# Table building and chunk inputs of a hybrid S5 layer: table buffers, store queue, three matrices kept, copies shared out

## The chip, the cores and the metric

The kernel runs on one NeuronCore of one Trainium2 chip. The metric is the device time of one execution in microseconds; three executions of the kernel before are given.

## The reference

The model has two layers over 1024 latent tokens and 256 context tokens of width 1024. The change lies in layer 0, in the S5 half of its mixer. It projects the normalised tokens to 768 channels `u` (48 groups of 16 channels) and runs a complex linear recurrence of 64 states for each group, once forwards and once backwards, over context and latent tokens together:

```python
lam_bar = jnp.exp(lam * step)
b_bar = ((lam_bar - 1.0) / lam)[..., None] * lax.complex(b_re, b_im)
bu = lax.complex(jnp.einsum('btgh,gph->btgp', u, b_bar.real),
                 jnp.einsum('btgh,gph->btgp', u, b_bar.imag))
...
_, s = lax.associative_scan(_linear_recurrence, (a, bu), axis=1)
return (jnp.einsum('btgp,ghp->btgh', s.real, c_re) - jnp.einsum('btgp,ghp->btgh', s.imag, c_im))
```

After it come a gated FNet mix of 256 channels, an output projection, and a second layer (pooling and a short convolution), which the change does not touch.

## The kernel before, in words

All instructions stand in the order in which the program writes them, engine by engine; there is no scheduler. fp32 products are made from three passes over values split in a high and a low part (`mm3`, L373); the low part `wlo` of a weight is made on VectorE, or on GpSimd, the high part `whi` on ScalarE (helper `act`, L243).

The recurrence is cut into chunks of 8 tokens: 160 chunk positions forwards and as many backwards. Three kinds of data are needed:

- **Input matrices** (`bl_task`, L507 to L531), twelve of them, each for 4 groups: VectorE makes `bl` in five operations on 128x512 from `bb` and `pwb` (the powers of `lam_bar`); the second half, `pe()`, is eight transposes on TensorE (L527), two copies on ScalarE to a slot `bltw`, and a store to DRAM `bltd` on GpSimd's queue (L530).
- **Output matrices** (`cl_task`, L533 to L575), twelve: VectorE makes `cl` in five operations on 128x576, and two stores `cld` go out (L556); the `pe()` half is 32 small matmuls into `pz` (L566), ScalarE's copies to `z`, and two small VectorE operations (`dg`, `z`). After every second task `z` is put in a list, and the next `flush()` stores it (L962, `zd`). There are two `z` buffers, so the first copy to the third `z` waits until the first `zd` store has landed.
- **Chunk inputs**: the projected `u` of channel block m is stored to DRAM `ud` by three DMAs on GpSimd's queue (L1021, L1024, L1025) and read back as `ub` in another layout.

The loop over m = 0 to 5 (L988) computes the six channel blocks and their context part `uc`. Inside its matmuls the hook calls `fill()` (L960 to L978) at chosen k. A `fill` flushes `z`, runs the `pe()` half of the table task two back, and starts the VectorE half of the next. So table number t+1's VectorE work and table t-1's TensorE work stand in the same place. The buffers of `bl` (2, with scratch `blp`) lie in pool `gt`, those of `cl` (2, with scratch `clp`) in pool `kt`. `cld` and `zd` stores go on `self.sq`, which is SyncE's queue until the loop over m has ended and GpSimd's from there.

Then comes `fx(0)` (the FNet projection, eight k steps), with `hook0` (L1063) at each k: at k other than 2 and 5 it runs one `bl_mm` and one `fill`. `bl_mm(i)` (L1033 to L1050) multiplies input matrix i (`blt`, loaded back from `bltd`) with the chunk inputs `ub`: for each of two parts one PSUM tile of 3 groups and one of 1 group, which ScalarE copies to the recurrence's state (128x480 and 128x160). It ends with `bl_load(i+3)`, two loads on SyncE's queue. `bl_mm` 0 to 5 write state half `va`, 6 to 11 half `vb`. `vb` lies where pool `kt` was, so its first write waits until the last table and `z` stores have landed.

VectorE then runs, for `va`, `tree(0)` (five levels) and six steps; `tree(1)` does it for `vb`, and after that a long run of dependent steps over both halves follows. TensorE projects further channel blocks beside it. The output stage (`yps`, L1205) needs the end of that chain.

Of the kernel before, what the change touches and what calls it, by code (L numbers as in the profile page):

```python
# [9 lines left out]
F32 = mybir.dt.float32  # L10
# [7 lines left out]
P = 128  # L18
# [176 lines left out]
class Builder:  # L195
# [218 lines left out]
    def s5_prelim(self, tp, s5s, raw):  # L414
# [88 lines left out]
                    self.act(self.acf[:, o[0], o[1]], pw[:, k, 8], scale=sc)  # L503
        return tables, inputs

    def bl_task(self, b, hf):

        nc = self.nc
        g4 = slice(8 * b + 4 * hf, 8 * b + 4 * hf + 4)
        bl = self.gt.tile([P, 2, 4, 16, 8], F32, tag="bl", name="bl", bufs=2)  # L510

        def dve():
            p = self.gt.tile([P, 4, 16, 8], F32, tag="blp", name="blp", bufs=1)
            B = [x[:, g4].unsqueeze(3).to_broadcast([P, 4, 16, 8]) for x in (self.bbs, self.bb[:, 0], self.bb[:, 1])]
            W = [self.pwb[:, i, g4].unsqueeze(2).to_broadcast([P, 4, 16, 8]) for i in range(3)]
            self.mul(p, B[0], W[0])
            self.mul(bl[:, 0], B[2], W[2])
            self.mul(bl[:, 1], B[1], W[1])
            self.sub(bl[:, 0], p, bl[:, 0])
            self.add(bl[:, 1], p, bl[:, 1])  # L520

        def pe():
            blt = self.slot("bltw").rearrange("p (r g n) -> p r g n", r=2, g=4)
            for ri in range(2):
                pt = self.ps("m", "pt")
                for g in range(4):
                    nc.tensor.transpose(pt[:, g * P:g * P + P], bl[:, ri, g].rearrange("p h s -> p (h s)"),  # L527
                                        self.c("ident"))
                self.act(blt[:, ri].rearrange("p g n -> p (g n)"), pt)
            nc.gpsimd.dma_start(self.bltd[b][:, :, 4 * hf:4 * hf + 4], blt)  # L530
        return dve, pe  # L531

    def cl_task(self, b, hf):  # L533

        nc = self.nc
        g0 = 8 * b + 4 * hf
        g4 = slice(g0, g0 + 4)
        cl = self.kt.tile([P, 2, 4, 144], F32, tag="cl", name="cl", bufs=2)

        def dve():  # L540
            p = self.kt.tile([P, 4 * 144], F32, tag="clp", name="clp", bufs=1)
            p4 = p.rearrange("p (g e h) -> p g e h", g=4, e=9)
            C = [x[:, g4].unsqueeze(2).to_broadcast([P, 4, 9, 16]) for x in (self.cbs, self.cb[:, 0], self.cb[:, 1])]
            W = [self.pwc[:, i, :, g4].rearrange("p e g -> p g e").unsqueeze(3).to_broadcast([P, 4, 9, 16])
                 for i in range(3)]
            c4 = cl.rearrange("p r g (e h) -> p r g e h", e=9)
            self.mul(p4, C[0], W[0])
            self.mul(c4[:, 0], C[2], W[2])
            self.mul(c4[:, 1], C[1], W[1])
            self.sub(c4[:, 0], p4, c4[:, 0])  # L550
            cf = cl[:, 1].rearrange("p g e -> p (g e)")
            self.stt(cf, p, -1.0, cf, ALU.mult, ALU.subtract)
            for d in range(2):
                r = slice(64 * d, 64 * d + 64)
                o = 16 * (1 - d)
                self.sq.dma_start(self.cld[b][r, :, 4 * hf:4 * hf + 4], cl[r, :, :, o:o + 128])  # L556

        def pe():
            pz = [self.ps("m", "pz"), self.ps("m", "pz")]
            for q in range(4):  # L560
                for ri in range(2):
                    for d in range(2):
                        r = slice(64 * d, 64 * d + 64)
                        o = slice(0, 128) if d == 0 else slice(16, 144)
                        w = self.bb[r, ri, g0 + q:g0 + q + 2].rearrange("p g h -> p (g h)")
                        nc.tensor.matmul(pz[d][32 * q:32 * q + 32, 0:128], w, cl[r, ri, q, o],  # L566
                                         start=(ri == 0), stop=(ri == 1), skip_group_check=True)
            if hf == 0 and b > 0:
                self.z = self.kt.tile([P, 2, 240], F32, tag="z", name="z", bufs=2)
            z = self.z[:, hf]  # L570
            self.act(z[:, 0:128], pz[1][:, 0:128])
            self.act(z[:, 128:240], pz[0][:, 16:128])
            dg = self.kt.tile([P, 16], F32, tag="dg", name="dg", bufs=2)
            self.stt(dg, self.c("eye16"), self.v("d", 2 * b + hf), pz[0][:, 0:16], ALU.mult, ALU.add)
            self.add(z[:, 112:128], z[:, 112:128], dg)  # L575
            if hf == 1:
                self.zq.append((b, self.z))
        return dve, pe


# [167 lines left out]
    def layer0(self, es):  # L748
        nc, tc, A = self.nc, self.tc, self.A
# [184 lines left out]
        tables, inputs = self.s5_prelim(xp, s5s, rawb)  # L934
        rest, self.inter = self.inter, []
        for x in rest:
            if not isinstance(x, int):
                x()
        tables(0)
        inputs = inputs()  # L940
        for _ in range(4):
            next(inputs)


# [3 lines left out]
            return hh[k], hlo[k]  # L948

        todo = []  # L950
        for b in range(6):
            todo += [(self.bl_task, b, 0), (self.bl_task, b, 1)]
        for b in range(6):
            todo += [(self.cl_task, b, 0), (self.cl_task, b, 1)]
        pend = []

        self.zq = []
        self.sq = nc.sync

        def flush():  # L960
            for b, z in self.zq:
                self.sq.dma_start(self.zd[b].rearrange("a p e -> p a e"), z)  # L962
            self.zq = []

        def fill():
            flush()
            if len(pend) == 2 or not todo:
                if pend:
                    pend.pop(0)()
            if todo:  # L970
                f, b, hf = todo.pop(0)
                t = f(b, hf)
                if f == self.cl_task and b + hf == 0:
                    self.add(self.cbs, self.cb[:, 0], self.cb[:, 1])
                t[0]()
                pend.append(t[1])
# [2 lines left out]

        def bl_load(i):  # L980
            b, hf = divmod(i, 2)
            blt = self.slot("blt").rearrange("p (r g n) -> p r g n", r=2, g=4)
            nc.sync.dma_start(blt, self.bltd[b][:, :, 4 * hf:4 * hf + 4])
            ub = self.slot("ub")[:, 0:768].rearrange("p (g j) -> p g j", g=4)
            nc.sync.dma_start(ub, self.ud[b][4 * hf:4 * hf + 4].rearrange("g h s j -> (h s) g j"))
            blq.append((blt, ub))

        for m in range(6):  # L988
# [11 lines left out]
            if m == 1:  # L1000
                tables(1)
                sx.close()
                self.gt = ax.enter_context(tc.tile_pool(name="gt", bufs=1))
                self.kt = kx.enter_context(tc.tile_pool(name="kt", bufs=1, side="right"))
                self.z = self.kt.tile([P, 2, 240], F32, tag="z", name="z", bufs=2)
                self.cb = self.kt.tile([P, 2, NG, 16], F32, name="cb")
                nc.sync.dma_start(self.cb, A["s5c"])
                self.cbs = self.kt.tile([P, NG, 16], F32, name="cbs")
# [4 lines left out]
            self.mm3([(pc[:, :TC], 0, TC)], hi, lo, lambda k: (chh[k], chl[k]), 8)  # L1013
            if m == 0:
                self.w_split(names[2])
                for _ in inputs:
                    pass
            else:
                fill()
# [14 lines left out]
        def bl_mm(i):  # L1034
            blt, ub = blq.pop(0)
            for ri in range(2):
                for g0, n in ((0, 3), (3, 1)):
                    ps = self.ps("m" if n == 1 else "acc", "vps")
                    for j in range(n):
                        g = g0 + j  # L1040
                        o = slice(160 * j, 160 * j + 160)
                        nc.tensor.matmul(ps[0:64, o], blt[:, ri, g, 0:64], ub[:, g, 0:160], start=True, stop=True)
                        nc.tensor.matmul(ps[64:128, o], blt[:, ri, g, 64:128], ub[:, g, 32:192][:, ::-1],
                                         start=True, stop=True)
                    c, gl = divmod(4 * i + g0, NH)
                    dst = v[c][:, :, ri, gl:gl + n].rearrange("p i g -> p g i")
                    src = ps[:, 0:160 * n].rearrange("p (g i) -> p g i", g=n)
                    self.act(dst, src)
            if i + 3 < 12:
                bl_load(i + 3)  # L1050

        blk = list(range(12))
        self.sq = nc.gpsimd

        def fx(ct, hook):
            x = self.slot("fx")
# [4 lines left out]
            return lambda: nc.gpsimd.dma_start(xd[:, ct], x)  # L1061

        def hook0(k):  # L1063
            if k not in (2, 5):
                bl_mm(blk.pop(0))
                fill()

        fx(0, hook0)()
# [63 lines left out]
        n = NSTEP - 1  # L1132
# [6 lines left out]
        for m in range(8, 16):  # L1139
            k = m - 8  # L1140
# [90 lines left out]
        for i in range(12):  # L1231
# [19 lines left out]
            if i == 9:  # L1251
                for j, op in enumerate((ALU.add, ALU.subtract)):
                    o = 512 * j
# [26 lines left out]
        for kt in range(5):  # L1280
# [3 lines left out]
            for i in range(ni):  # L1284
                o = 512 * i if kt < 4 else 512
# [18 lines left out]
        for kt in range(4):  # L1304
            hi, lo = self.w_take(("dft", kt))
            self.w_split(("dft", kt + 1) if kt < 3 else ("glu", 0))
            for i in range(2):
                cs_ = slice(512 * i, 512 * i + 512)
                for ct in range(2):
                    cc = slice(128 * ct, 128 * ct + 128)  # L1310
                    zhh, zll = zh[:, i, kt, cc], zl[:, i, kt, cc]
                    o = pa[2 * i + ct]
# [513 lines left out]
```

## Time and profile before

| what | value |
|---|---|
| median of three executions | 913.28 us (912.3 to 913.72) |
| the profiled execution | 915.5 us |
| span of its trace | 913.7 us |
| granted TensorE clock, mean | 0.976 |
| TensorE busy | 864.6 us (95%) |
| VectorE busy | 673.0 us (74%) |
| ScalarE busy | 343.4 us (38%) |
| GpSimd busy | 94.2 us (10%) |

The engine shares are means over stages with different limits. The stage that the change touches runs from about 75 us (first channel block) to about 218 us (start of `tree(1)`); the page's 40 slices of 22.8 us each show TensorE there at 7 to 9 tenths, and the DMA engines at 9 tenths from 137 to 206 us. In every view, times count from the start of the span, and an idle time in square brackets stands with what ended it.

### The profile page before, as it was taken

Reading aid. Unit: us, or ns where it says so; the run is one execution under the profiler, and the core shown is the slowest. Engines: PE = TensorE matmul, PEld = TensorE weight load, DVE = VectorE, ACT = ScalarE, POOL = GpSimd, SP = SyncE. Lnnn points to the kernel's source line nnn. Section 1 sums busy time; section 2 is a strip of 40 time slices with the busy share of each in tenths; the row PEclk is TensorE's granted clock in tenths of the full one; section 3 lists DMA queues with packets and bytes.
Section 4 is the critical chain, followed back from the end, with each engine's and each line's share of the span. In section 5 each row is a group of like instructions: output and inputs, shape, how many; then the busy total and the mean of one; then the engine's idle time right before and its main releaser. Section 6 shows DMA issues by size and latency. Waiting matters only on the chain.

```text
span 913.7 us, 14101 instructions
## 1 busy us (share of the span) xinstructions
PE 864.6 (95%) x5312; PEld 708.2 (78%) x5312; DVE 673.0 (74%) x1740; ACT 343.4 (38%) x597; POOL 94.2 (10%) x91
## 2 busy tenths in 40 slices
PE   9997998989999967799999999999999999999995
PEld 4666886768777747787888999877778888878995
DVE  7777997857999996755457376698887776785354
ACT  4547341446112109843433143542222333263111
POOL 0002321221221212300016001000000000000000
PEclk9899999999999988999999999999999999999997
DMA  9642779993455565951255303102111111233022
GB/s 349 267 173 74 221 249 268 228 364 128 162 208 190 192 220 157 310 162 54 69 188 179 134 29 93 47 13 74 63 45 50 46 47 56 79 130 151 1 94 93
DMA packets 62212, 129.16 MB, mean 141 GB/s; under 512 B 5760, under 2 KB 32560, under 8 KB 62016
## 3 DMA queue, kind: packets, MB, share of 16 engines
q1 hardware_dynamic: 55280, 104.45, 34.4%
q0 software_dynamic: 6864, 23.81, 8.4%
q8 instruction: 42, 0.69, 0.3%
q14 instruction: 26, 0.21, 0.1%
HBM read 100.03 MB, written 28.21 MB: 140 GB/s over the span
## 4 chain that ended last, share of the span: by engine, by line
PE 64%; DVE 22%; ACT 6%; DMA 5%; issue 1%; SPq 1%; DVEq 0%; POOL 0%; ACTq 0%
PE acc L373 32%; PE acc L1743 19%; DVE va L218 11%; DVE vb L218 2%; DMA ub<-ud 2%; PE acc L883 2%; ACT vb L243 2%; PE yps L1205 1%; DMA mt<-zd 1%; PE pt L527 1%; DVE xt L218 1%; PE rsb L694 1%; PE uc L373 1%; DVE wlo L218 1%; PE pps L1652 1%
## 5 line engine op out<-in xcount | busy, mean ns | idle before, releaser
L373 PE MATMUL acc<-hh,whi 128*128 128x512 f32 (+1 forms) x352 | 113.3, 388 | 3.9 <-ACT whi L243 3.9
L373 PE MATMUL acc<-hl,whi 128*128 128x512 f32 (+1 forms) x352 | 109.9, 379 | 0.0
L373 PE MATMUL acc<-hh,wlo 128*128 128x512 f32 (+1 forms) x352 | 109.4, 377 | 0.0
L373 PEld LDWEIGHTS acc<-hh,whi 128*128 128x128 f32 x352 | 63.6, 192 | 19.3 <-issue 5.1
L373 PEld LDWEIGHTS acc<-hh,wlo 128*128 128x128 f32 x352 | 66.1, 191 | 13.6 <-DVE wlo L218 0.5
L373 PEld LDWEIGHTS acc<-hl,whi 128*128 128x128 f32 x352 | 66.0, 191 | 13.3
L243 ACT ACTIVATE whi<-hh 128x512 fp32r<-128x512 f32 (+4 forms) x44 | 26.9, 629 | 110.4 <-DVE hh L218 97.1
L243 ACT ACTIVATE whi<-raw 128x512 fp32r<-128x512 f32 (+3 forms) x65 | 51.7, 799 | 37.1 <-DMA raw<-in_win 16.7
L1743 PE MATMUL acc<-th,whi 128*128 128x512 f32 x160 | 63.3, 396 | 1.2 <-DVE hl L218 1.2
L218 DVE TENSOR_TENSOR va<-va 128x48 f32<-128x48 f32 (+1 forms) x258 | 62.8, 244 | 0.4
L1743 PE MATMUL acc<-tl,whi 128*128 128x512 f32 x160 | 62.4, 390 | 0.3 <-DVE tl L218 0.3
L1743 PE MATMUL acc<-th,wlo 128*128 128x512 f32 x160 | 62.3, 389 | 0.0
L218 DVE TENSOR_TENSOR wlo<-raw,whi 128x512 fp32r<-128x512 f32 (+3 forms) x57 | 48.4, 854 | 16.5 <-ACT whi L243 16.4
L239 DVE SCALAR_TENSOR_TENSOR xl<-acc,adac,xl 128x256 f32<-128x256 f32 (+1 forms) x48 | 27.3, 570 | 38.5 <-PE acc L373 36.4
L218 DVE TENSOR_TENSOR wlo<-hh,whi 128x512 fp32r<-128x512 f32 (+4 forms) x44 | 30.4, 690 | 24.9 <-ACT whi L243 24.9
L1743 PE MATMUL acc<-hh,whi 128*128 128x512 f32 x120 | 47.5, 396 | 0.0
L1743 PE MATMUL acc<-hh,wlo 128*128 128x512 f32 x120 | 46.8, 390 | 0.3 <-DVE wlo L218 0.3
L1743 PE MATMUL acc<-hl,whi 128*128 128x512 f32 x120 | 46.7, 389 | 0.0
L373 PE MATMUL acc<-th,hl 128*128 128x256 f32 (+1 forms) x144 | 45.9, 319 | 0.5 <-DVE hl L218 0.5
L373 PE MATMUL acc<-th,hh 128*128 128x256 f32 (+1 forms) x144 | 46.3, 321 | 0.1
L373 PE MATMUL acc<-hh,wh 128*128 128x256 f32 (+1 forms) x144 | 46.2, 321 | 0.0
L373 PE MATMUL acc<-hh,wl 128*128 128x256 f32 (+1 forms) x144 | 46.1, 320 | 0.0
(295 smaller groups left out, 2124.0 us busy)
## 6 DMA issues: line engine op xcount, KB each, us to landing
raw<-in_ada SPq DMA_DIRECT2D x44, 512.0 KB, 5.9
raw<-in_win SPq DMA_DIRECT2D x38, 512.0 KB, 3.7
raw<-in_wout SPq DMA_DIRECT2D x16, 512.0 KB, 3.8
bltd<-bltw POOLq DMA_DIRECT2D x12, 512.0 KB, 5.0
blt<-bltd SPq DMA_DIRECT2D x12, 512.0 KB, 7.7
cl<-cld POOLq DMA_DIRECT2D x12, 512.0 KB, 6.5
cld<-cl SPq DMA_DIRECT2D x18, 256.0 KB, 4.9
ub<-ud SPq DMA_DIRECT2D x12, 384.0 KB, 6.9
```

Of the source, the lines that this page charges most:

```text
L218: (eng or self.nc.vector).tensor_tensor(out, a, b, op=op)
L239: self.nc.vector.scalar_tensor_tensor(out, a, s, b, op0=op0, op1=op1)
L243: self.nc.scalar.activation(out, a, func, **kw)
L373: self.nc.tensor.matmul(p, a[:, w], b[:, c0:c1], start=(j == 0 and i == 0), stop=(last and i == 2))
L527: nc.tensor.transpose(pt[:, g * P:g * P + P], bl[:, ri, g].rearrange("p h s -> p (h s)"), self.c("ident"))
L694: self.nc.tensor.matmul(p2[:, P * i:P * i + P], self.ones, dg[:, i], start=True, stop=True)
L883: nc.tensor.matmul(acc[m][h], a[:, w], b[:, 512 * h:512 * h + 512], start=(k == 0 and i == 0), stop=(k == 7 and i == 2))
L1205: nc.tensor.matmul(ps[:, o], sy[:, ri, g], cl[:, ri, g], start=False, stop=(ri == 1))
L1652: nc.tensor.matmul(ps, pwt[:, i], st[i][:, 4 * h:4 * h + 4], start=True, stop=True)
L1743: nc.tensor.matmul(ps, x[:, sl], y, start=bool(new and k == 0 and i == 0), stop=(k == 3 and i == 2), skip_group_check=True)
```

## The change

1. `tables(0)`, the six ScalarE copies that make `pwb`, moves from ahead of the loop over m to the end of m = 0, behind the split of the next weight; only two of the seven remaining input operations (four before) run ahead of the loop.
2. Both kinds of table take their buffer from one helper, `tab()`: three places in pool `kt` and, for every fourth table, one in `gt` (not for the last five). Both use one scratch `tabp`.
3. All `cld` and `zd` stores go on GpSimd's queue: 18 `cld` and 3 `zd` stores leave SyncE's.
4. The input matrices are made in the order 3 to 11, then 0, 1, 2. The last three stay in their slots: three `bltd` stores and three `blt` loads go.
5. `hook0` runs `bl_mm` at k = 0 to 5 and `fill` at every k but 1.
6. The twelve 128x160 copies to `vb` move from ScalarE to VectorE, where they stand between the levels of `tree(0)`.

```diff
+    def tab(self):
+        self.ntab += 1
+        if self.gt is not None and self.ntab % 4 == 0:
+            return self.gt.tile([P, 1152], F32, tag="tab", name="tab", bufs=1)
+        return self.kt.tile([P, 1152], F32, tag="tab", name="tab", bufs=3)
...
-        bl = self.gt.tile([P, 2, 4, 16, 8], F32, tag="bl", name="bl", bufs=2)
+        bl = self.tab()[:, 0:1024].rearrange("p (r g h s) -> p r g h s", r=2, g=4, h=16)
...
+            if 2 * b + hf < 3:
+                self.blts[2 * b + hf] = blt
...
-            nc.gpsimd.dma_start(self.bltd[b][:, :, 4 * hf:4 * hf + 4], blt)
+            if 2 * b + hf > 2:
+                nc.gpsimd.dma_start(self.bltd[b][:, :, 4 * hf:4 * hf + 4], blt)
...
-        cl = self.kt.tile([P, 2, 4, 144], F32, tag="cl", name="cl", bufs=2)
+        cl = self.tab().rearrange("p (r g e) -> p r g e", r=2, g=4)
...
-                self.sq.dma_start(self.cld[b][r, :, 4 * hf:4 * hf + 4], cl[r, :, :, o:o + 128])
+                nc.gpsimd.dma_start(self.cld[b][r, :, 4 * hf:4 * hf + 4], cl[r, :, :, o:o + 128])
...
-        tables(0)
         inputs = inputs()
-        for _ in range(4):
+        for _ in range(2):
             next(inputs)
...
-        for b in range(6):
-            todo += [(self.bl_task, b, 0), (self.bl_task, b, 1)]
+        for i in (3, 4, 5, 6, 7, 8, 9, 10, 11, 0, 1, 2):
+            todo.append((self.bl_task, *divmod(i, 2)))
...
-                self.sq.dma_start(self.zd[b].rearrange("a p e -> p a e"), z)
+                nc.gpsimd.dma_start(self.zd[b].rearrange("a p e -> p a e"), z)
...
+                if len(todo) < 5:
+                    self.gt = None
...
-            blt = self.slot("blt").rearrange("p (r g n) -> p r g n", r=2, g=4)
-            nc.sync.dma_start(blt, self.bltd[b][:, :, 4 * hf:4 * hf + 4])
+            blt = self.blts.pop(i, None)
+            if blt is None:
+                blt = self.slot("blt").rearrange("p (r g n) -> p r g n", r=2, g=4)
+                nc.sync.dma_start(blt, self.bltd[b][:, :, 4 * hf:4 * hf + 4])
...
                 self.w_split(names[2])
+                tables(0)
...
-                    self.act(dst, src)
+                    if n == 1 and i > 5:
+                        nc.vector.tensor_copy(dst, src)
+                    else:
+                        self.act(dst, src)
...
-        self.sq = nc.gpsimd
...
         def hook0(k):
-            if k not in (2, 5):
+            if k < 6:
                 bl_mm(blk.pop(0))
+            if k != 1:
                 fill()
```

Three places show how the instructions now stand. On ScalarE, at the first channel blocks, `pwb` are the copies of `tables(0)`, `ut` and `utc` those of a channel block, `whi` the high part of the weight for m = 2. Before:

```order
L243 ACTIVATE pwb<-pw 64x8x48 x6
L243 ACTIVATE ut<-acc 128x512 [waits PE_49] x2
L243 ACTIVATE whi<-raw 128x1024 [waits DMAHW7_49,PE_49]
L243 ACTIVATE utc<-uc 128x256 [waits PE_49]
L243 ACTIVATE ut<-acc 128x512 x2
L243 ACTIVATE pwc<-pw 64x432 x6
L243 ACTIVATE acf<-pw 128x48 x4
```

And with the change:

```order
L243 ACTIVATE ut<-acc 128x512 [waits PE_49] x2
L243 ACTIVATE whi<-raw 128x1024 [waits DMAHW7_49,PE_49]
L243 ACTIVATE pwb<-pw 64x8x48 x6
L243 ACTIVATE utc<-uc 128x256 [waits PE_49]
L243 ACTIVATE ut<-acc 128x512 x2
L243 ACTIVATE pwc<-pw 64x432 x6
L243 ACTIVATE acf<-pw 128x48 x4
```

The six `pwb` copies stand behind the weight's high part, and the ones for the step after (`pwc`, `acf`) are where they were.

On GpSimd's queue, around the fifth channel block's three stores (`ud`) and the first `zd` store, with the change (before, this queue held only `bltd` and `ud` stores until the loop over m had ended):

```order
L567 DMA cld_85<-tab 128x4x128 [waits DMASW1_49,DVE_49]
L567 DMA cld_85<-tab 128x4x128 [waits DMASW2_49]
L567 DMA cld_85<-tab 128x4x128 [waits DMASW3_49,DVE_49]
L567 DMA cld_85<-tab 128x4x128 [waits DMASW4_49]
L1037 DMA ud_100<-ut 1024x1x128 [waits DMASW5_49,Activation_49]
L1040 DMA ud_100<-utc 1024x1x32 [waits DMASW6_49,Activation_49]
L1041 DMA ud_100<-utc 1024x1x32 [waits DMASW7_49]
L972 DMA zd_90<-z 128x2x240 [waits DMASW0_49]
L567 DMA cld_86<-tab 128x4x128 [waits DMASW1_49,DVE_49]
```

The first `zd` store stands behind the `cld` stores of the fourth output matrix and behind the three `ud` stores; before, it was SyncE's, behind loads of `blt`, `ub` and a weight.

On VectorE, at `tree(0)`, with the change (`tr` is the tree's scratch, `vps` a PSUM tile of `bl_mm`):

```order
L1106 COPY acf_2128<-acf_2128 128x48 [waits DVE_49]
L1065 COPY vb<-vps 128x160 [waits DMASW4_49,DMASW5_49,DMASW3_49,DMASW6_49,DMASW1_49,DMASW7_49,DMASW0_49,PE_49]
L1065 COPY vb<-vps 128x160 [waits PE_49] x3
L218 TENSOR_TENSOR tr<-va,acf 128x768 x2
L218 TENSOR_TENSOR va<-va,tr 128x16x48 [waits DVE_49] x2
L1065 COPY vb<-vps 128x160 [waits PE_49] x2
L218 TENSOR_TENSOR tr<-va,acf_2125 128x384 [waits DVE_49]
L218 TENSOR_TENSOR tr<-va,acf_2125 128x384
L218 TENSOR_TENSOR va<-va,tr 128x8x48 [waits DVE_49] x2
L1065 COPY vb<-vps 128x160 [waits PE_49] x2
L218 TENSOR_TENSOR tr<-va,acf_2126 128x192 [waits DVE_49]
L218 TENSOR_TENSOR tr<-va,acf_2126 128x192
```

Before, the tree's levels followed one another without the `vb` copies, which were all ScalarE's; the first copy now waits for the stores that lie in the place of `vb`, with the whole tree behind it.

## Rows read from the trace of the kernel before

**Rows 1.** Windows by stage: busy PE, PEld, DVE, ACT, POOL; PEclk, DMA share, GB/s.

```profile
185.00:200.00 15.00, 13.34 (x186) 11.07 (x188) 6.29 (x32) 7.10 (x15) 3.40 (x5) 1.00 1.06 375
...
230.00:330.00 100.00, 100.00 (x595) 74.98 (x594) 100.00 (x617) 17.65 (x38) 20.86 (x13) 1.00 0.58 204
```

**Rows 2.** Chain that ended last, 195 to 350: start, us, what.

```profile
195.69 8.95 DMA ub<-ud
```

**Rows 3.** Timeline of TensorE: start, us, instructions, idle before and its releaser.

```profile
346.73 1.23 PE L1205 MATMUL yps<-cl,sy 128*128 128x128 f32 x4 [12.30 <-ACT sy L243]
```

**Rows 4.** Waits, 75 to 235: in total, times, longest us.

```profile
DVE cl L218 <- DMA cld<-cl: 12.4, 5, 5.4
```

**Rows 5.** Timeline of ScalarE.

```profile
76.71 5.66 ACT L243 ACTIVATE pwb<-pw 64x384 f32<-64x384 f32 x6
...
162.22 0.76 ACT L243 ACTIVATE z<-pz 128x128 f32<-128x128 f32 x4 [13.79 <-DMA zd<-z]
...
204.65 13.57 ACT L243 ACTIVATE vb<-vps 128x480 f32<-128x480 f32 x24 [3.04 <-DMA ub<-ud]
```

**Rows 6.** Timeline of TensorE after 80.5.

```profile
84.61 0.74 PE L373 MATMUL acc<-hh,whi 128*128 128x512 f32 x2 [3.87 <-ACT whi L243]
...
89.16 0.63 PE L373 MATMUL acc<-hh,whi 128*128 128x512 f32 x2
...
93.36 0.82 PE L527 MATMUL pt<-cst,bl 128*128 128x128 f32 x6
```

**Rows 7.** One window after that pause, columns as in rows 1.

```profile
86.00:87.00 1.00, 1.00 (x4) 0.81 (x4) 1.00 (x2) 0.98 (x3) 1.00 (x3) 0.50 1.07 299
```

**Rows 8.** Timeline of SyncE's queue.

```profile
155.67 0.43 SPq L962 DMA_DIRECT2D zd<-z  x1
...
208.48 0.36 SPq L985 DMA_DIRECT2D ub<-ud  x1
```

**Rows 9.** Timeline of GpSimd's queue.

```profile
180.49 1.54 POOL L556 DMA_DIRECT2D cld<-cl  x2 [9.73 <-issue]
...
197.39 0.73 POOL L962 DMA_DIRECT2D zd<-z  x1 [1.75 <-issue]
```

**Rows 10.** Timeline of VectorE.

```profile
89.81 0.69 DVE L218 TENSOR_TENSOR blp<-bbs,pwb 128x512 f32<-128x512 f32 x1 [1.27 <-ACT acf L243]
...
146.34 0.75 DVE L239 SCALAR_TENSOR_TENSOR cl<-clp,cl 128x576 f32<-128x576 f32 x1
...
190.37 1.43 DVE L218 TENSOR_TENSOR cl<-cb,pwc 128x576 f32<-128x576 f32 x2 [5.40 <-DMA cld<-cl]
...
200.73 1.83 DVE L218 TENSOR_TENSOR tr<-va,acf 128x768 f32<-128x768 f32 x2 [1.08 <-ACT va L243]
...
209.56 0.26 DVE L218 TENSOR_TENSOR va<-va,acf 128x96 f32<-128x96 f32 x1
...
213.75 0.45 DVE L218 TENSOR_TENSOR va<-va 128x48 f32<-128x48 f32 x2
218.26 1.83 DVE L218 TENSOR_TENSOR tr<-vb,acf 128x768 f32<-128x768 f32 x2 [4.05 <-ACT vb L243]
```

**Rows 11.** Vb copies by form: count, busy us, mean ns.

```profile
L243 ACT ACTIVATE vb<-vps 128x480 f32<-128x480 f32 x12 | 12.5, 1041 | 3.0 <-DMA ub<-ud 3.0
L243 ACT ACTIVATE vb<-vps 128x160 f32<-128x160 f32 x12 | 5.8, 487 | 0.0
```

**Rows 12.** Small VectorE operation that reads PSUM, 150 to 200.

```profile
L239 DVE SCALAR_TENSOR_TENSOR dg<-cst,vec,pz 128x16 f32<-128x16 f32 x9 | 2.0, 227 | 5.4 <-ACT z L243 5.4
```

**Rows 13.** DMA issues, 60 to 240: count, KB each, median us to landing.

```profile
cld<-cl SPq DMA_DIRECT2D x18, 256.0 KB, 4.9
...
cld<-cl POOLq DMA_DIRECT2D x6, 256.0 KB, 7.6
```

**Rows 14.** Timeline of TensorE, start of the last input multiplication.

```profile
213.89 0.32 PE L1042 MATMUL vps<-ub,blt 128*64 128x160 f32 x1
```

**Rows 15.** Tile of the chunk inputs, 205 to 218: durations, first and last start.

```profile
L1043 PE MATMUL vps<-ub,blt x64: 299/299/350, 205.7 to 216.0; 128*64 128x160 f32 x64
```

More of the change, by code (lines that the diff above doesn't have):

```diff
@@ L509, in bl_task @@
         g4 = slice(8 * b + 4 * hf, 8 * b + 4 * hf + 4)
-        bl = self.gt.tile([P, 2, 4, 16, 8], F32, tag="bl", name="bl", bufs=2)
+        bl = self.tab()[:, 0:1024].rearrange("p (r g h s) -> p r g h s", r=2, g=4, h=16)
         def dve():
-            p = self.gt.tile([P, 4, 16, 8], F32, tag="blp", name="blp", bufs=1)
+            p = self.kt.tile([P, 576], F32, tag="tabp", name="blp", bufs=1)[:, 0:512]
+            p = p.rearrange("p (g h s) -> p g h s", g=4, h=16)
             B = [x[:, g4].unsqueeze(3).to_broadcast([P, 4, 16, 8]) for x in (self.bbs, self.bb[:, 0], self.bb[:, 1])]
@@ L537, in cl_task @@
         g4 = slice(g0, g0 + 4)
-        cl = self.kt.tile([P, 2, 4, 144], F32, tag="cl", name="cl", bufs=2)
+        cl = self.tab().rearrange("p (r g e) -> p r g e", r=2, g=4)
         def dve():
-            p = self.kt.tile([P, 4 * 144], F32, tag="clp", name="clp", bufs=1)
+            p = self.kt.tile([P, 576], F32, tag="tabp", name="clp", bufs=1)
             p4 = p.rearrange("p (g e h) -> p g e h", g=4, e=9)
@@ L957, in layer0 @@
         self.zq = []
-        self.sq = nc.sync
+        self.blts = {}
         def flush():
             for b, z in self.zq:
-                self.sq.dma_start(self.zd[b].rearrange("a p e -> p a e"), z)
+                nc.gpsimd.dma_start(self.zd[b].rearrange("a p e -> p a e"), z)
             self.zq = []
@@ L1003, in layer0 @@
                 self.gt = ax.enter_context(tc.tile_pool(name="gt", bufs=1))
+                self.ntab = 0
                 self.kt = kx.enter_context(tc.tile_pool(name="kt", bufs=1, side="right"))
```

## The prediction

> **What bounds the kernel now.** I read the chain of waits first. From 195.69 it runs over 8.95 us of a DMA's landing [rows 2] into ScalarE's copies to `vb` [rows 5], and from there over VectorE's tree and steps. Two views say that VectorE's chain carries everything up to the output stage: in the window 230 to 330 VectorE is busy 100 of 100 us [rows 1], and TensorE stands idle for 12.30 us before the first output matmul at 346.73, waiting for the end of that chain [rows 3]. So the start of `tree(1)`, 218.26 [rows 10], passes on one for one: a microsecond gained there is one gained at 346.73, and TensorE has 12.3 us to spare in between. That is the number to forecast.
>
> Next I read who waits for whom before it. Two kinds of store are waited for, since two buffers of each were not enough. VectorE's `cl` waited 12.4 us for `cld` stores, five times [rows 4]. ScalarE's wait for a `zd` store is the anchor of my sum: the third `z` pair is copied at 162.22, after 13.79 us idle [rows 5], when the first `zd` store has landed. That store was issued at 155.67 on SyncE's queue [rows 8] and took 6.55 us. From 162.22 (call it T) to `tree(1)` it is 56.0 us.
>
> **The change part by part.**
>
> *The `tables(0)` move: nothing before 93 us.* Six copies of 5.66 us [rows 5] hold the weight's high part back, and TensorE waits 3.87 us for it [rows 6]. With the change the weight comes first and TensorE starts some 4 us earlier, at about 80.6. But the first table operation on VectorE starts at 89.81, when `acf` is done [rows 10]: ScalarE has the same copies to make up to there in either order. The first transposes stand behind the fifth k step and needed that table at 93.36 [rows 6]. Five k steps of 1.4 us from 80.6 end at 87.6, so TensorE now waits some 5.3 us there instead. The pause moves and does not go. After the pause of before the clock was at 0.50 (1.2 GHz) in 86 to 87 [rows 7]; its first six pairs of matmuls took 4.55 us (84.61 to 89.16), the next nine 4.20 (to 93.36), so 0.47 each and 2.8 for six [rows 6]. A pause at 88 to 93 puts that 1.7 us behind the first table rather than ahead. Between 0 and 1.7 us of it reach the `cl` stage; I take the middle, 0.8.
>
> *The four buffers.* The 12.4 us of `cl` waiting go, all five waits. Cover: a table is five operations of 0.75 us [rows 10], so with four buffers one is wanted again after three others, 11 us, and stores land in 7.6 us [rows 13]. What is late next is `z`, which keeps two buffers.
>
> *The first `zd` store, on GpSimd's queue.* It stands behind the stores of the fourth output matrix and three `ud` stores. That matrix's last VectorE operation ends at 147.1 (146.34 and 0.75 [rows 10]). Two issues take 1.54 us on this queue [rows 9], and five stand ahead, 3.9: issue at about 151.0, against 155.67. GpSimd's last `zd` store before `vb`, issued at 197.39 [rows 9], let the first `vb` copy start at 204.65 [rows 5]: 7.26 us. So T becomes 158.3, and 159.1 with the 0.8 from the clock. Bounds: 6.55 us of landing and no clock loss give 157.6; all of the 1.7 and one more cld pair ahead 161.5.
>
> The Trainium skill's "DMA: Bandwidth & Descriptors", section "Issuing engine by pattern", puts simple loads and stores on Sync and calls that path generally faster than GpSimd's, which speaks against this part. The trace bears it out for the landing alone: `cld` stores took 4.9 us from SyncE and 7.6 from GpSimd [rows 13]. By the rule alone, with every store issued when it is now, T would come 2.7 us later, at 164.9, and the time would be 916.0; that is the second rival's end below.
>
> What decides against that here is the issue time: 4.7 us earlier, less 0.7 of longer landing, is 4.0 us gained before the clock's 0.8.
>
> *From T to the last `z` store.* Before, 162.22 to 197.39 is 35.2 us. In it VectorE waited 5.40 us for a `cld` store at 190.37 [rows 10]; that goes. What TensorE waits there for chunk inputs may stay; I give 0.8 back, an estimate: 30.6 us. Should TensorE rather than that wait set the pace, only 2.4 of the 5.4 are won.
>
> *From the last `z` store to `tree(1)`.* Landing, 7.26 us, as before; it frees the place of `vb`. Before, 24 copies of ScalarE follow back to back, 13.57 us [rows 5], and `tree(1)` starts as they end, with VectorE idle 4.05 us [rows 10]. Afterwards ScalarE has twelve of 1041 ns, 12.5 us [rows 11], beside VectorE, which has more: four small copies, then `tree(0)` with the other eight in it, then the steps. `tree(0)` and steps are 200.73 to 214.20, 13.5 us, of which the steps begin at 209.56 [rows 10]. A 128x160 copy of VectorE from PSUM is in no row: not under the 227 ns of its 128x16 operation that reads PSUM [rows 12], not over ScalarE's 487 ns [rows 11] (as bounds, though neither excludes more); nearest in engine is the former, and for ten times the columns I take 300: 3.6 us in all, ends 2.7 and 5.8. Sum 17.1 us. The tree that ran free between 200.73 and 204.65 now stands behind the landing: that is the price of moving the copies.
>
> *Kept matrices and removed DMAs.* Three stores and three loads of 512 KB are 3.1 MB, 8.4 us of the 375 GB/s that the full engines moved [rows 1]. No path gets shorter by itself, but from 185 to 200 the DMA share was 1.06 [rows 1], and the last chunk inputs, issued at 208.48 [rows 8], queue in it. That issue was 46.3 us after T; without the 5.40 it is T+41, and I count nothing more for it. `bl` order and `hook0` reorder the same work: nothing.
>
> *Sum.* 159.1 + 30.6 + 7.3 + 17.1 = 214.1, against 218.26: 4.1 us less. The sum is made on the profiled execution (span 913.7, 915.5 in all); I take the difference from the median, 913.28, which lies 2.2 below it: **909.2**. By the bounds: 157.6 and 2.7 us of copies give 6.5 less, 161.5 and 5.8 us of copies leave 0.5 more; the usual course is 905.5 to 911.4.
>
> **The rivals.**
>
> *The last loads decide (slower).* The last `ub` load waits for `fx`'s buffer, and so for the `xd` store. Before, it was issued at 208.48 [rows 8], and the last input multiplication started at 213.89 [rows 14], 5.4 us later: on its landing. Only four copies and `tree(1)` stood behind. Now part of the chain of `va` does: matmuls 2.1 (213.89 to 216.0 [rows 15]), one copy 0.3, the tree's last level some 0.8, and six steps 4.6 (209.56 to 214.20 [rows 10]), 7.8 in all. If that load keeps its time, `tree(1)` starts at 221.7, 3.4 later: 916.7. It decides from a start of the last multiplication after 210.5, where the forecast has 159.1 + 41 + 5.4 = 205.5 or a little later. For it: the DMA share of 1.06. Against it: 8.4 us of DMA work less, and the `fx` matmuls freed of the 5.40 us. A start at 209 to 212 gives 911.9 to 914.9, no change.
>
> *GpSimd's queue holds the first `zd` store (slower).* One queue in order: a `cld` store that waits for VectorE holds `ud` and `zd` behind it. If it is issued after 155 rather than 151, T is over 163 and every microsecond more costs one: 914 to 917, with a landing of 10 us the same. For it: the longer landing, 2.7 us on a `cld` store [rows 13]. Against it: an issue costs 0.77 us, and five of them end before SyncE's turn came.
>
> *The pause at 80.5 was worth its length.* If VectorE could begin earlier than `acf`, 3.9 us of TensorE's would come on top: 905.3. The row on `acf` speaks against it.
>
> *More is won.* If the first store lands before its next writer comes, the `z` wait vanishes and T is set by VectorE's tables, at 153 to 156 (it had `cl` waits of 12.4 us to lose [rows 4]); T + 55 is 208 to 211: 903 to 906.
>
> **How the numbers follow.** A measurement tells 0.2%, 1.8 us, from no change. Forecast 0.48, nearly all faster; more won 0.14 and the early pause 0.03, faster; last loads 0.22, half of it within 1.8 us, half slower; GpSimd's queue 0.13, a third within 1.8 us, the rest slower. Faster 0.64, same 0.17, slower 0.19. The range reaches from the middle of the larger gain into the last loads: 904.5 to 915.5.
>
> **What would show it.** Right: no `cl` wait for `cld`; ScalarE's `z` waits for `zd` shorter, the third pair copied at 157 to 160; a pause of 5 us on TensorE before the first transposes at 93, low clock after it; `tree(1)` at 213 to 215 with VectorE not idle before it; all else the same to the end. Wrong: the first `zd` store issued after 155, VectorE idle at the small `vb` copies or late in `tree(0)`, or TensorE's 12.3 us before the output stage gone, so that `tree(1)` no longer counts one for one.

## The result, and the profile after

The changed kernel takes 922.73 us (median of four, 920.01 to 924.1) against 913.5 for the kernel before, run beside it: ratio 1.0095, 95% interval 1.0072 to 1.0119. It is slower by about 9 us, where 4 less was forecast, and outside the range. The profiled execution took 922.78 us with a span of 920.7, which is 7.0 more than the span before; the profiled execution before lay 2 us above its median, so the profiles show less than the 9 us.

Five pieces of the chain that ended last, in the changed kernel, and one of the kernel before (start, us, what):

```profile
148.26 7.57 DMA zd<-z
...
169.91 15.17 DMA ub<-ud
...
204.61 4.77 DMA ub<-ud
...
217.60 0.46 DVE vb L1065
...
219.39 2.46 DVE va L218
```

```profile
179.07 6.44 DMA ub<-ud
```

The first `zd` store landed 7.57 us after its issue, as forecast. Then comes a landing of 15.17 us, of the chunk inputs of `bl_mm(3)`; before, the same load landed in 6.44. VectorE's small copies and steps follow near the end of the stage.

TensorE's idle times in the changed kernel:

```profile
90.61 1.94 PE L537 MATMUL pt<-cst,tab 128*128 128x128 f32 x8 [5.12 <-issue]
...
185.22 0.50 PE L1058 MATMUL vps<-ub,blt 128*64 128x160 f32 x1 [9.63 <-DMA ub<-ud]
...
351.33 1.22 PE L1224 MATMUL yps<-cl,sy 128*128 128x128 f32 x4 [15.62 <-ACT sy L243]
```

The pause at 80 is now one of 5.12 us that ends at 90.61. At 185.22 TensorE has waited 9.63 us for `ub`; before, the same multiplication started at 185.65, one k step further on, so this wait undoes what had been gained ahead of it. The last row answers to [rows 3]: the output stage starts 4.60 us later than before.

The stretch from 165 to 185 (busy PE, PEld, DVE, ACT, POOL; PEclk, DMA share, GB/s), changed and then before:

```profile
165.00:185.00 20.00, 10.60 (x146) 8.03 (x132) 11.11 (x19) 6.36 (x14) 9.26 (x12) 0.85 0.93 260
```

```profile
165.00:185.00 20.00, 19.68 (x272) 15.53 (x271) 18.51 (x35) 10.08 (x23) 5.87 (x8) 1.00 0.88 219
```

TensorE is busy 10.60 of 20 us instead of 19.68, and its mean granted clock is 0.85 instead of 1.00.

SyncE's queue in the changed kernel, where the two loads for `bl_mm(3)` are issued behind a weight load:

```profile
145.31 23.77 SPq L323 DMA_DIRECT2D raw<-in_ada  x2
169.17 0.65 SPq L997 DMA_DIRECT2D blt<-bltd  x1
169.91 1.39 SPq L999 DMA_DIRECT2D ub<-ud  x1
```

GpSimd's queue, the same stretch and its last rows:

```profile
168.44 1.50 POOL L567 DMA_DIRECT2D cld<-tab  x2 [2.07 <-DVE tab L239]
169.94 0.90 POOL L1037 DMA_DIRECT2D ud<-ut  x1
170.74 0.97 POOL L1040 DMA_DIRECT2D ud<-utc  x1
171.52 1.06 POOL L1041 DMA_DIRECT2D ud<-utc  x1
172.70 1.53 POOL L567 DMA_DIRECT2D cld<-tab  x2
174.22 0.73 POOL L972 DMA_DIRECT2D zd<-z  x1
178.96 1.50 POOL L567 DMA_DIRECT2D cld<-tab  x2 [4.01 <-DVE tab L239]
...
200.92 0.72 POOL L972 DMA_DIRECT2D zd<-z  x1 [3.83 <-issue]
...
219.32 2.40 POOL L218 TENSOR_TENSOR wlo<-raw,whi 128x1024 fp32r<-128x1024 f32 x1 [15.35 <-ACT whi L243]
```

Seven `cld` and `zd` stores of 240 or 256 KB and the three `ud` stores of the last channel block are issued between 168.44 and 180.5, just as the loads go out. What each queue moved from 165 to 185 (packets, MB, share of 16 engines' time; software is GpSimd's queue, hardware SyncE's), changed and then before:

```profile
q0 software_dynamic: 922, 3.02, 58.8%
q1 hardware_dynamic: 1505, 2.15, 33.7%
```

```profile
q1 hardware_dynamic: 4610, 3.57, 68.7%
q0 software_dynamic: 240, 0.79, 18.4%
```

GpSimd's queue went from 0.79 to 3.02 MB and took 58.8% of the engines' time, SyncE's fell from 68.7% to 33.7%.

ScalarE and VectorE at the two places of the sum, in the changed kernel:

```profile
155.94 0.76 ACT L243 ACTIVATE z<-pz 128x128 f32<-128x128 f32 x4 [9.74 <-DMA zd<-z]
```

```profile
87.90 0.69 DVE L218 TENSOR_TENSOR blp<-bbs,pwb 128x512 f32<-128x512 f32 x1 [5.48 <-ACT acf L243]
...
205.37 0.98 DVE L1065 COPY vb<-vps 128x160 f32<-128x160 f32 x3 [2.18 <-DMA zd<-z]
...
219.39 2.45 DVE L218 TENSOR_TENSOR va<-va,acf 128x96 f32<-128x96 f32 x1
...
225.36 1.82 DVE L218 TENSOR_TENSOR tr<-vb,acf 128x768 f32<-128x768 f32 x2
```

The third `z` pair is copied at 155.94 (162.22 before [rows 5]), and `tree(1)` starts at 225.36 (218.26 before [rows 10]). From the first copy to `vb` to `tree(1)` it is 20.0 us, against 13.6 before. The first copy itself comes 0.7 us later than before (205.37 against 204.65 [rows 5]), so of the 7.1 us by which `tree(1)` is later nearly all lie behind it.

### The profile page after: what moved, and what is told of

It reads as the page before. It is cut to its first block, busy times and chain, and to the rows that moved or that the text cites. A ratio compares the mean times of both kernels' runs of the same rounds, so it can differ in the third digit from the quotient of the medians.

```text
span 920.7 us, 14092 instructions
## 1 busy us (share of the span) xinstructions
PE 861.2 (94%) x5312; PEld 706.9 (77%) x5312; DVE 675.2 (73%) x1752; ACT 341.1 (37%) x585; POOL 107.2 (12%) x109
## 4 chain that ended last, share of the span: by engine, by line
PE 67%; DVE 22%; DMA 5%; ACT 5%; issue 1%; POOL 0%; SPq 0%; DVEq 0%; ACTq 0%
PE acc L373 33%; PE acc L1762 19%; DVE va L218 11%; DVE vb L218 3%; PE vps L1058 2%; DMA ub<-ud 2%; PE acc L894 2%; PE yps L1224 1%; DMA mt<-zd 1%; PE pt L537 1%; PE uc L373 1%; DVE xt L218 1%; DMA zd<-z 1%; PE pps L1671 1%; PE yps L1222 1%
## 5 line engine op out<-in xcount | busy, mean ns | idle before, releaser
L373 PEld LDWEIGHTS acc<-hl,whi 128*128 128x128 f32 x352 | 65.4, 189 | 13.0
L1762 PE MATMUL acc<-th,whi 128*128 128x512 f32 x160 | 63.3, 396 | 1.2 <-DVE hl L218 1.2
L218 DVE TENSOR_TENSOR va<-va 128x48 f32<-128x48 f32 (+1 forms) x258 | 53.6, 209 | 0.4
L1224 PE MATMUL yps<-cl,sy 128*128 128x128 f32 x192 | 33.8, 305 | 17.0 <-ACT sy L243 15.6
```

The source lines that it names most:

```text
L218: (eng or self.nc.vector).tensor_tensor(out, a, b, op=op)
L373: self.nc.tensor.matmul(p, a[:, w], b[:, c0:c1], start=(j == 0 and i == 0), stop=(last and i == 2))
L1224: nc.tensor.matmul(ps[:, o], sy[:, ri, g], cl[:, ri, g], start=False, stop=(ri == 1))
L1762: nc.tensor.matmul(ps, x[:, sl], y, start=bool(new and k == 0 and i == 0), stop=(k == 3 and i == 2), skip_group_check=True)
```

## Experiments

Times are medians; each ratio is to the kernel before, run beside it on the same chip, with its 95% interval. For the changed kernel it is 1.0095. The chips differ, so two experiments are compared by their ratios; 0.1% is 0.9 us.

**1. A weight load less in front of the loads.** `w_split(names[7])` moves from the start of `fx(0)` to its fifth k step:

```diff
-            if ct == 0:
-                self.w_split(names[7])
...
+            if k == 4:
+                self.w_split(names[7])
```

> The split of the second FNet weight, whose end frees the buffer for a weight load that stands on SyncE's queue ahead of the loads for bl_mm(3), moves from the start of fx(0) to its fifth k step. In the changed kernel those loads were issued at 169.17 and 169.91, landed 15 us later, and TensorE waited 9.63 us for them until 185.22. Theory A (the weight load holds SyncE's queue): they are issued when bl_mm(0) ends, at about 165, land after the usual 7 us, the wait goes, and the time falls by 8 to 10 us, to 913 to 915. Theory B (GpSimd's stores take the DMA engines meanwhile): issued at 165, they still take 12 to 15 us, TensorE waits 4 us or more, and the time is 917 to 921.

922.37 us, ratio 1.0091 (1.0060 to 1.0122): no change. SyncE's queue, then TensorE:

```profile
164.69 0.64 SPq L997 DMA_DIRECT2D blt<-bltd  x1
165.42 1.14 SPq L999 DMA_DIRECT2D ub<-ud  x1
169.26 0.54 SPq L997 DMA_DIRECT2D blt<-bltd  x1
169.92 1.87 SPq L999 DMA_DIRECT2D ub<-ud  x1
```

```profile
187.48 0.50 PE L1058 MATMUL vps<-ub,blt 128*64 128x160 f32 x1 [7.55 <-DMA ub<-ud]
```

The loads for `bl_mm(3)` went out at 164.69 and came in time, but those for `bl_mm(4)`, issued at 169.26 and 169.92, took until 187.4. The wait moved one `bl_mm` on. Theory A falls as the main cause; the landing is the problem, not the issue.

**2. `hook0`'s old places for `bl_mm`.** `if k not in (2, 5)` instead of `if k < 6`.

> Only hook0 runs bl_mm where it did before the change (every k but 2 and 5); the fills stay. bl_mm(3) then stands one k step and one fill later, some 4 to 5 us. Theory C (its new place is too early for loads that cannot come sooner): TensorE's wait of 9.63 us falls to 4 to 6, and the time by 2 to 4 us, to 918.5 to 921. If the place does not matter (the work between only moves): 922 to 924.

923.47 us, 1.0103 (1.0074 to 1.0132). TensorE still waits 9.23 us, until 186.83. Theory C falls: the loads are late at either place.

**3. Three pairs of stores 25 us earlier.**

```diff
-                nc.gpsimd.dma_start(self.cld[b][r, :, 4 * hf:4 * hf + 4], cl[r, :, :, o:o + 128])
+                t = 2 * b + hf
+                for i in ([] if t in (7, 8, 9) else [t]) + ([t + 7] if t < 3 else []):
+                    nc.gpsimd.dma_start(self.cld[i // 2][r, :, 4 * (i % 2):4 * (i % 2) + 4], cl[r, :, :, o:o + 128])
```

> The six stores of output matrices 7, 8 and 9 are left out; stores of the same size into their places go out with matrices 0, 1 and 2 instead, some 25 us earlier, so the output matrices of these three are wrong. The loads for bl_mm(3), issued at 169.2, then have only two cld and three ud stores beside them on GpSimd's queue instead of six and three. Theory B (GpSimd's stores take the DMA engines): they land after 8 to 11 us instead of 15, TensorE's wait of 9.63 falls to 3 to 6 us, the time to 916 to 919. Theory A (only the time of issue counts): issue and wait as in the changed kernel, 921 to 924.

915.95 us, 1.0028 (1.0008 to 1.0048): 0.67% of the loss of 0.95% is gone, some 6 us, at the lower end of what theory B expected. The queues from 165 to 185, and the landing of the chunk inputs:

```profile
q1 hardware_dynamic: 2587, 3.42, 52.2%
q0 software_dynamic: 560, 1.80, 38.9%
```

```profile
DMA to landing us min/median/max: 4.5/7.6/9.0
```

No load of chunk inputs takes over 9.0 us (18.7 in the changed kernel, 13.4 before), and TensorE has no wait there, although the loads are issued 4 us later (173.3) and the first `zd` store, behind more stores, lands 4 us later (`z` at 160.08). The two queues move 5.2 MB in the stretch, as much as in the changed kernel; only GpSimd's part is smaller. Theory B stands.

**4. All twelve input matrices through DRAM**, made in the order 0 to 11, with their stores and loads.

> All twelve input matrices are stored and loaded, made in the order 0 to 11, as before the change. Theories A and B: the loads for bl_mm(3) stand where they stood, so the wait stays at 8 to 11 us; the six DMAs come back, three of them in the 30 us ahead of fx(0), for 0 to 3 us: 922 to 926. If keeping them is what brought the loads together in the busy stretch (a rival), the wait shrinks and the time is below 920.

922.49 us, 1.0099 (1.0072 to 1.0127), with a wait of 9.36 us. Keeping three matrices gains and costs nothing that shows in the changed kernel.

**5. The small copies back on ScalarE.** `if False` in place of `if n == 1 and i > 5`.

> The twelve 128x160 copies to vb go back to ScalarE; all else as changed. In the changed kernel the first copy to vb starts at 205.37 and tree(1) at 225.36, 20.0 us later; before, 13.6 us lay between (24 copies of ScalarE end to end, tree(0) beside them). Theory D (the copies chain tree(0) to the landing of the last z store): tree(1) comes 13 to 15 us after the first copy, the time falls by 5 to 7 us, to 915.5 to 918. Rival (the last chunk inputs set the end, whoever copies): tree(1) stays 19 to 20 us behind, 921 to 924.

921.41 us, 1.0067 (1.0045 to 1.0089). Its six times lie in two groups, 916.8 and 916.9, and four from 921.4 to 921.8, with a mean granted clock of 0.977 to 0.978 in the first and 0.971 to 0.973 in the second; the profile is of the first, and why there are two was not found. ScalarE and VectorE in it:

```profile
206.12 13.53 ACT L243 ACTIVATE vb<-vps 128x480 f32<-128x480 f32 x24 [2.90 <-DMA zd<-z]
```

```profile
219.69 1.83 DVE L218 TENSOR_TENSOR tr<-vb,acf 128x768 f32<-128x768 f32 x2 [3.08 <-ACT vb L243]
```

From the first copy to `tree(1)` it is 13.57 us again. Theory D holds in the profile; the median gains 1.3 us where 5 to 7 were expected, 0.28% by the ratios, whose intervals overlap.

**6. `tables(0)` back in front.**

> tables(0) goes back ahead of the loop over m. The prediction's step: the pause of TensorE only moves (3.9 us at 80 before, 5.1 at 90.6 in the changed kernel), so the time stays within 1.5 us, 921 to 924.5. If the move is worth its pause: 925 to 928.

920.2 us, 1.0078 (1.0061 to 1.0095). TensorE's pause is 3.83 us at 81.93 and the later one is gone. The intervals overlap: the move is worth nothing that shows.

**7. Stores ahead of `fx(0)` on SyncE's queue again** (`self.sq`, as in the kernel before).

> The cld and zd stores issued before fx(0) go back to SyncE's queue; those from fx(0) on stay on GpSimd's. Theory B (what counts is what is stored from 165 to 185, beside the loads): nearly the same DMAs fall there, TensorE's wait in the early bl_mm stays 6 us or more, 919 to 925. Rival (the whole move of stores to GpSimd's queue costs): the wait goes and the time is 915 to 918.

916.42 us, 1.0033 (1.0015 to 1.0052). The rival's number came, though the wait did not go, and my reading of theory B was wrong: not nearly the same DMAs fall on GpSimd's queue in that stretch.

```profile
q1 hardware_dynamic: 4654, 4.22, 74.9%
q0 software_dynamic: 374, 1.19, 20.7%
```

GpSimd's queue has 1.19 MB instead of 3.02, SyncE's 4.22 instead of 2.15, together 5.4 MB instead of 5.2. TensorE waits 4.1 us, until 181.22.

**8. Experiments 3 and 5 together.**

> The early stores of the third experiment (matrices 7, 8 and 9 of the output kind wrong, as there) and ScalarE's small copies together. If theories B and D name two separate costs, their gains add: 915.95 less 5 to 7 is 909 to 911, faster than the kernel before. If they are one cost seen twice: 914 to 916.

914.17 us, 1.0004 (0.9990 to 1.0019): together they take back the whole loss. The number lies in the range that stood for one cost seen twice, so the time does not tell the two theories apart. The profiles do: `z` came 2.5 us later in this execution than in that of experiment 3 (162.54 and 160.08), and counted from there `tree(1)` starts 6.4 us earlier (53.5 us instead of 59.9).

**9. Experiments 7 and 5 together.**

> The seventh and fifth experiment together: stores ahead of fx(0) on SyncE's queue, ScalarE's small copies; four buffers, three kept matrices, the tables move and hook0 stay. If both costs are real and separate: 916.4 less 2 to 5, so 911.5 to 914.5, level with the kernel before or a little faster. If the copies cost nothing once the loads come in time: 916 to 917.

910.65 us, 0.9952 (0.9935 to 0.9969): faster than both kernels. ScalarE, TensorE and VectorE:

```profile
156.36 0.76 ACT L243 ACTIVATE z<-pz 128x128 f32<-128x128 f32 x4 [8.23 <-DMA zd<-z]
...
199.60 13.62 ACT L243 ACTIVATE vb<-vps 128x480 f32<-128x480 f32 x24 [2.81 <-DVE va L218]
```

```profile
179.07 0.32 PE L1059 MATMUL vps<-ub,blt 128*64 128x160 f32 x1 [3.07 <-DMA ub<-ud]
...
341.63 1.22 PE L1226 MATMUL yps<-cl,sy 128*128 128x128 f32 x4 [11.90 <-ACT sy L243]
```

```profile
213.25 1.83 DVE L218 TENSOR_TENSOR tr<-vb,acf 128x768 f32<-128x768 f32 x2 [3.05 <-ACT vb L243]
```

The wait for chunk inputs is 3.07 us, `tree(1)` starts at 213.25, 5.0 before the kernel before, and the output stage 5.1 before it.

**10. Only the six stores of output matrices 7, 8 and 9 on SyncE's queue.**

```diff
-                nc.gpsimd.dma_start(self.cld[b][r, :, 4 * hf:4 * hf + 4], cl[r, :, :, o:o + 128])
+                q = nc.sync if 2 * b + hf in (7, 8, 9) else nc.gpsimd
+                q.dma_start(self.cld[b][r, :, 4 * hf:4 * hf + 4], cl[r, :, :, o:o + 128])
```

> Of the changed kernel only the six stores of output matrices 7, 8 and 9 go on SyncE's queue, at their own time; same bytes, same stretch, same results. Theory B1 (two queues share the DMA engines, and GpSimd's large packets take most of it from the loads): GpSimd moves some 1.5 MB less from 165 to 185, the loads for the early bl_mm land in 7 to 11 us, the wait falls to 5 us or less, 916 to 919.5. Theory B2 (the volume in that stretch decides, whichever queue): the loads wait behind these stores in their own queue and the wait stays at 8 to 11 us, 921 to 924.

918.93 us, 1.0041 (1.0026 to 1.0055): inside B1's range.

```profile
q1 hardware_dynamic: 4096, 3.10, 56.4%
q0 software_dynamic: 552, 1.77, 38.2%
```

```profile
184.62 0.50 PE L1059 MATMUL vps<-ub,blt 128*64 128x160 f32 x1 [5.95 <-DMA ub<-ud]
```

The same bytes, on the loads' own queue and ahead of them, leave the longest landing of chunk inputs at 9.7 us. But the loads stand behind these stores and are issued at 176.9 instead of 169.2, so they come hardly earlier (184.62 against 185.22). The wait is 5.95 us, a little over the bound given. The third `z` pair came 3.1 us later in this execution (159.03), so the start at 184.62 shows less than was gained: in experiment 11, where it came at 156.31, TensorE waits 6.14 us until 182.12, 3.1 us earlier than in experiment 5's profile (185.27). So the other queue lengthens the landing, and part of the wait stays as the loads' place in their own queue. The volume does not explain it: the stretch moves 5.2 MB in the changed kernel and in experiment 3, and 5.4 in experiment 7.

**11. Experiments 10 and 5 together.**

> The experiment before this one and ScalarE's small copies. Under B1 and theory D (copies): 912 to 916. Under B2: 919 to 922, as with ScalarE's copies alone.

915.9 us, 1.0020 (1.0003 to 1.0037): 0.2% less than experiment 10, which the overlapping intervals do not settle.

**12. Experiments 9 and 1 together.**

> The first of this call with the split of the second FNet weight at the fifth k step, so that no weight load stands ahead of the loads for bl_mm(3). Theory A as a smaller, second cost: the loads are issued at about 167 instead of 172.5, the rest of TensorE's wait there goes, 1 to 3 us faster than the first of this call: 909.5 to 913. If the engines are the limit: the same as it.

909.97 us, 0.9953 (0.9935 to 0.9971): not to be told from experiment 9, though the loads go out at 170.0 instead of 171.3.

**13 and 14. Two buffers for each kind of table**, in the changed kernel and in the version of experiment 9.

> The changed kernel with two buffers for each kind of table, as before the change. Theory F (the buffers bring the stores together, and that is part of the loss): VectorE waits for cld stores again, which spaces them, the loads for the early bl_mm land in under 12 us, and the time is 916 to 920. If the buffers only help: the waits come on top, 923 to 927.

924.44 us, 1.0116 (1.0090 to 1.0143), with a wait of 10.56 us for chunk inputs. Theory F falls: the buffers don't make the loss.

> The faster version (stores ahead of fx(0) on SyncE's queue, small copies on ScalarE, 910.65) with two buffers for each kind of table. What the prediction gave to the buffers, 5.4 us at most on the path: 913 to 916. If the first z store, not the buffers, sets the pace (now issued without input loads ahead of it on SyncE's queue): 910 to 912.

913.65 us, 0.9990 (0.9973 to 1.0007), and VectorE waits again:

```profile
DVE cl L218 <- DMA cld<-cl: 4.7, 6, 1.7
```

So the four buffers are worth about 3 us by the medians where the loads come in time. In the two profiles only 0.8 of it stands at the start of the output stage (342.45 against 341.63); the rest lies behind it, where the buffers have no part that these views show.

## Why the prediction was wrong

**The step that failed** is "from T to the last `z` store": 30.6 us were forecast, 45.0 came (155.94 to 200.92). I took out the wait that went, 5.40 us, and asked only whether the *last* loads would come later. Two things were wrong with that. First, ten DMAs of GpSimd's queue now run in the 12 us in which the *first* loads of `fx(0)` go out, and I had priced the moved stores at their issue, 0.77 us each, and at their own landing. What they cost was the landing of the loads: 15 us instead of 6.4. The sentence "I count nothing more for it" is where it should have been counted, since [rows 1] already showed a DMA share of 1.06 from 185 to 200, and the stretch from 165 to 185 stood at 0.88.

Second, the wait taken out of the sum was not there to be won. From the third `z` pair to the last `z` store (columns as above; the kernel before, the changed kernel, experiment 8):

```profile
162.20:197.40 35.20, 33.21 (x432) 26.41 (x432) 24.82 (x53) 17.19 (x40) 8.55 (x12) 0.98 0.95 277
```

```profile
156.00:201.00 45.00, 34.68 (x452) 28.04 (x453) 24.79 (x53) 19.19 (x44) 13.87 (x19) 0.89 0.88 258
```

```profile
162.50:197.50 35.00, 34.63 (x451) 28.30 (x452) 24.64 (x52) 19.19 (x44) 9.30 (x12) 0.91 0.84 259
```

TensorE is busy 33.2 of the 35.2 us before, so 30.6 was less than its own work there. In experiments 3 and 8, where it has no wait for loads, the stretch takes 35.2 and 35.0 us: no `cl` wait is left, and nothing is won against the 35.2 of before. The prediction named the case, that TensorE sets the pace, and still gave it 2.4 us. So of the 14.4 us that the step missed, some 4.5 are TensorE's own work and some 10 the late loads.

How two queues share the engines, the rows show: from 165 to 185 GpSimd's 922 packets of 3.3 KB took 58.8% of 320 us of engine time (16 engines for 20 us), 204 ns each, and SyncE's 1505 packets of 1.4 KB 33.7%, 72 ns each. The Trainium skill's "DMA: Bandwidth & Descriptors", section "Queues, rings and completion order", says that an engine goes round the queues that have work, a packet at a time. If its packets are those that the profile counts, which no run here shows, and both queues always have work, that would give the queue of the larger packets 74% of what the two take, an estimate from the two times; 64% was measured, which agrees in direction. Experiments 3, 7 and 10 show that the stores in GpSimd's queue lengthen the landings; that it is by packets is argued. The rule of the same page of the Trainium skill that the prediction set aside, plain loads and stores from Sync (section "Issuing engine by pattern"), held here (experiment 7, 1.0033 against 1.0095), though not through the stores' own landing, 5.4 us at the median in the changed kernel against 4.9 from SyncE before.

**Right:** the pause moved and did not go (5.12 us until 90.61; 5.3 until 93 forecast), and experiment 6 shows no gain. VectorE's first table began 1.9 us earlier than I had it, since `acf` came earlier. The `cl` waits are all gone. The first `zd` store was issued at 148.26 and landed in 7.57 (151.0 and 7.26 forecast), so T came at 155.94, 3.2 earlier than the sum had it. But the gain did not need GpSimd's queue: in experiment 9 SyncE issues it at 150.59 and T is 156.36; the three `blt` loads no longer stand ahead of it, which I take to be why, though no run shows it alone. In the changed kernel kept matrices and `hook0` are worth nothing that shows (experiments 4 and 2); in experiment 9's version they were not tried.

**From the last `z` store to `tree(1)`:** 24.4 us forecast and 24.4 measured (200.92 to 225.36), by errors that cancel, which is luck. The landing took 4.45 us, not 7.26; the 7.26 was read up to a copy whose wait [rows 5] puts down to chunk inputs, not to the store. The rest took 20.0, not 17.1: the small copies are longer than the 300 ns I took,

```profile
L1065 DVE COPY vb<-vps 128x160 f32<-128x160 f32 x12 | 4.5, 435 | 3.4 <-DMA zd<-z 2.2 <-PE vps L1059 1.1
```

435 ns each, near the upper end of my bounds; VectorE waits 1.1 us for matmuls between them; and one step took 2.45 us instead of 0.26, of which the last section tells. That moving them loses against ScalarE's 13.6 us was in the sum and was hidden by the gains beside it. Without the stretched step moving them costs 4.2 us. In all four pairs of runs with and without them the median is lower with ScalarE's copies, by 0.2 to 0.8%; the intervals are apart only for experiments 7 and 9. The profiles show it more evenly, counted from the third `z` pair:

| pair: with VectorE's copies, with ScalarE's | to `tree(1)`, us | to the output stage, us |
|---|---|---|
| changed kernel, experiment 5 | 69.4, 63.3 | 195.4, 191.7 |
| experiments 3, 8 | 59.9, 53.5 | 185.9, 181.9 |
| experiments 7, 9 | 63.3, 56.9 | 189.2, 185.3 |
| experiments 10, 11 | 65.7, 60.3 | 191.7, 188.6 |

So the copies cost 5.4 to 6.4 us at `tree(1)` and 3.1 to 4.1 at the output stage, whether the loads come late or not.

**One for one:** `tree(1)` is 7.1 us later, the output stage 4.6, the end 7.0. Of the first difference 2.2 us are the stretched step, which before fell behind the start of `tree(1)`. Of the last, 1.0 lie in the 72 us after the output stage's start, where TensorE's work takes 65.4 us instead of 63.9 at a granted clock of 0.92 instead of 0.94, and 1.4 in a stretch at 1.2 GHz that the kernel before does not have. These 2.4 are not the change's: in experiment 6 the output stage starts at 351.53, and what follows takes 566.2 us, against 567.0 before and 569.4 here. The window of that stretch in the changed kernel, columns as above, shows a granted clock of 0.50 with TensorE busy all the time:

```profile
425.00:428.00 3.00, 3.00 (x9) 2.33 (x8) 2.96 (x8) 0.48 (x1) 0.00 (x0) 0.50 0.00 0
```

**The rivals:** the one that names GpSimd's queue had the side but less than half of the size (914 to 917), and its mechanism, a late first `zd` store, did not happen. "The last loads decide" looked at the right resource and mostly at the wrong loads. It came close all the same: the chain that ended last runs over the chunk inputs issued at 204.61, and VectorE's last small copy waits 0.65 us for their matmuls. Its condition was misread, too: 210.5 is the start at which it cancels the gain, and by its own 7.8 us it would pass the forecast's 214.1 from 206.3 on. And 905.5 to 911.4, called the usual course, does not follow from the bounds beside it, which give 906.8 to 913.8.

## What to carry to other kernels

A store that nobody waits for is not free when it is moved: lay its transfer time, and that of all others moved with it, over the stretch in which it will now run, and look for loads that are due there. Putting stores on a second queue takes them out of the order that kept them from the loads; if the engines are full, keep the stores in the loads' own queue, or move them to a stretch where nothing is due. Before taking a wait out of a sum, look at what the busiest engine does in that stretch: its work is the least that can be left. And work taken from one engine (here 5.8 us of ScalarE's copies) should not be put into a chain of another that already starts at the same event.

## What the runs showed of the hardware

VectorE's one step at 219.39 took 2.45 us, where the same form takes 0.26, and it lies beside GpSimd's `wlo` on 128x1024, at 219.32 for 2.40 us. In the kernel before, an operation at 220.00 lay likewise beside such a `wlo`, VectorE and then GpSimd:

```profile
220.00 3.16 DVE L218 TENSOR_TENSOR vb<-vb,tr 128x768 f32<-128x768 f32 x1
```

```profile
219.17 3.17 POOL L218 TENSOR_TENSOR wlo<-raw,whi 128x1024 fp32r<-128x1024 f32 x1 [16.71 <-ACT whi L243]
```

The next operation of its form took 0.96 us. The pair recurs in the profiles of experiments 1, 3, 7 and 10 (a step of 2.41 to 2.44 us beside a `wlo` of 2.39 to 2.40). So a long GpSimd operation held one VectorE operation until it ended.
